# Retention's query-times-state product: two fp32 matmuls replaced by six fp32r matmuls on split operands

## The chip, the cores and the metric

The kernel runs on one core of a Trainium2 chip. TensorE (PE) multiplies matrices from SBUF into PSUM, VectorE (DVE) and ScalarE (ACT) do elementwise work on SBUF and PSUM, GpSimd (POOL) does elementwise work on SBUF, and SyncE (SP) mostly issues DMAs. Each engine runs its own instructions in order. The metric is the device time in microseconds (us); lower is better.

## The reference, cut to what matters

Two layers, each a mixer and a convolutional feed-forward network. Layer 0 mixes by a gated delta net, layer 1 by retention, which is the part that concerns us: 1024 tokens in 8 chunks of 128, 4 heads, keys of 256 and values of 512.

```python
scores = jnp.einsum('bhncd,bhnmd->bhncm', q, k) * dmask[None, :, None]
intra = jnp.einsum('bhncm,bhnmv->bhncv', scores, v)

def step(state, inp):
    q_n, k_n, v_n = inp
    o = jnp.einsum('bhck,bhkv->bhcv', q_n, state) * xi[None, :, :, None]
    state = (state * gamma_c[None, :, None, None]
             + jnp.einsum('bhck,bhcv->bhkv', k_n * zeta[None, :, :, None], v_n))
    return state, o

o = _unchunk_heads(intra + jnp.moveaxis(inter, 0, 2))
o = _standardize(o, 1e-6).reshape(b_, s, H * dv)
o = o * jax.nn.silu(gate.astype(F32))
return o.astype(h.dtype) @ w_out
```

The state is 256 x 512 per head. The product of the change is `q_n` (128 x 256) times `state`, once per chunk and head, from the second chunk on (the state starts at zero).

## The kernel before

**Split products.** Nearly all products are taken as three fp32r matmuls: an operand x is split into a high part (`act.activation(dst_h, src, AF.Copy)`, which rounds to fp32r, L89) and a low part (`eng.tensor_tensor(dst_l, src, dst_h, ALU.subtract)`, L90; `eng` is VectorE unless given), and low x high, high x low and high x high are summed in PSUM. `split` (L88) does this. A few products stay plain fp32 matmuls.

**Retention, layer 1.** Two streams share TensorE. `core(h)` runs through the chunks of head h; `ret_fill` makes the values V of the heads one half (four chunks) after the other (`ret_v`) and then the first two block products of the output projection (`proj_gen`). The planner `run` (L727) writes TensorE's order out by hand: a stream that yields a number is not continued before so much planned time has passed, a core step goes before fill, and the constants in `RL` are these pauses. `pm` and `ptr` pin each matmul and transpose behind the one before. The other engines' instructions take program order among what is ready.

**One chunk n of `core`**, in program order:

- the next state `Sn` (two halves j of 128 x 512): three fp32r matmuls each (`sc<-vv,kz`), then VectorE adds the decayed old state (L1957; for n = 0 it copies, L1955)
- `ret_front` for chunk n+1: scores (`mm<-qk`), transposes of k, `kz` (zeta times k, split, L1921 and L1922), the masked scores `sT` (L1924) and their split `sThl`; it also keeps the slices of q that the chunk needs
- a pause `RL["p"]`, then the output `po` (`sc<-vv,sThl`: three fp32r matmuls; for n > 0 also `sc<-Sr,qk`: two plain fp32 matmuls of q times the state `St`)
- `ret_back` starts as a stream of its own: statistics of `po` (L1977, L1979, L1980), a power on GpSimd (L1981), the normalised `on` (L1985), after a pause `RL["b"]` four transposes (`mm<-cst,on`), times the gate (L2006), and stores; from n = 4 on also four GpSimd operations that combine output blocks (L2017). For n < 4 it also starts a gain step (GpSimd, L2055 and L2056) for the residual input
- a pause `RL["c"]`

`po` and the state products take PSUM banks from the tag `sc`, which has two.

**The ring `qkv`** is an SBUF tag of 20 places of 128 x 512. A chunk's V takes two of them (`vv`, high and low). `take("qkv", 2)` in `ret_v` holds the fill back, in the plan, until two places are free, and `give("qkv", 2)` in `core` gives a chunk's two back; the count starts from `free["qkv"] = 20`. The output projection's blocks and weights use the same tag.

`load_qk` brings q and k of a head from DRAM into the tags `aux` and `auh`, each half as two tiles or two slices of one tile of 128 x 512.

Of the kernel before, what the change touches and what calls it, by code (L numbers as in the profile page):

```python
# [9 lines left out]
F32 = mybir.dt.float32  # L10
F32R = mybir.dt.float32r
# [4 lines left out]
P = 128  # L16
D = 1024
S = 1024
KT = D // P
HALF = 512  # L20
NCH = S // P
GH = 8
RH = 4
# [10 lines left out]
def trunk_kernel(ctx: ExitStack, tc, A):  # L34
# [6 lines left out]
    dr = ctx.enter_context(tc.tile_pool(name="dr", bufs=1, space=bass.MemoryType.DRAM))  # L41

    BUFS = {"hTa": 8, "hTb": 8, "qkv": 20, "aux": 4, "auh": 8, "lane": 4, "cv": 4, "ada": 1,
            "wr": 2, "wh": 2, "wl": 2, "t2": 3, "sm": 14, "sm2": 6, "st": 8, "s8": 6, "S": 6, "qx": 3, "fs": 1, "xT": 2}

    def tl(tag, shape, dt=F32, name=None):
        return sb.tile(shape, dt, tag=tag, name=name or tag, bufs=BUFS[tag])

    def two(tag, dt=F32, name=None):
        if tag in ("qkv", "auh"):  # L50
            return tl(tag, [P, HALF], dt, name), tl(tag, [P, HALF], dt, name)
        t = tl(tag, [P, 2, HALF], dt, name)
        return t[:, 0], t[:, 1]
# [7 lines left out]
    def mm_tile():  # L61
        return ps.tile([P, HALF], F32, tag="mm", name="mm", bufs=2)

    def sc_tile():
        return ps.tile([P, HALF], F32, tag="sc", name="sc", bufs=2)
# [16 lines left out]
    def hs(half):  # L82
        return slice(half * HALF, (half + 1) * HALF)
# [4 lines left out]
    def split(dst_h, dst_l, src, eng=dve):  # L88
        anchor["sp"] = act.activation(dst_h, src, AF.Copy)  # L89
        eng.tensor_tensor(dst_l, src, dst_h, ALU.subtract)  # L90
# [488 lines left out]
    xT = {}  # L579
# [118 lines left out]
    U, DT, R, St = {}, {}, {}, {}  # L698
# [6 lines left out]
    def pq(inst, cost):  # L705
        if pin[0] is not None:
            tc.add_manual_dep(inst.ins, pin[0].name,
                              mybir.DependencyInfo(mybir.DependencyClass.NoSync, mybir.DependencyReason.DATA),
                              reason="issue order")
        pin[0] = inst.ins  # L710
        clk[0] += cost
# [3 lines left out]
    def pm(out, lhsT, rhs, start=True, stop=True, cost=None):  # L715
        pq(pe.matmul(out, lhsT, rhs, start=start, stop=stop), cost or COST[out.shape[-1]])  # L716

    def ptr(out, src):
        pq(pe.transpose(out, src, ident), 0.109)

    def after_ev(*names):
        return ("ev", names)

    def emit(name, lat=0.0):
        events[name] = clk[0] + lat
# [43 lines left out]
    free = {"qkv": 20 - 2 * (len(first) - 1), "lane": 4, "aux": 0, "auh": 8, "t2": 3, "xT": 2}  # L769
# [6 lines left out]
    def give(tag, n):  # L776
        free[tag] += n
# [461 lines left out]
    for p in range(4):  # L1239
        q = p & 2  # L1240
# [668 lines left out]
    def ret_front(h, n, q, k):  # L1909
        s4 = slice(n % 4 * P, (n % 4 + 1) * P)  # L1910
        qh, kh = q[n // 4], k[n // 4]
        r = {}
        pk = mm_tile()
        p1 = pk[:, 2 * P:3 * P]
        for j in range(2):
            pm(p1, kh[j][:, s4], qh[j][:, s4], start=(j == 0), stop=(j == 1))
        if n < NCH - 1:
            for j in range(2):
                ptr(pk[:, j * P:(j + 1) * P], kh[j][:, s4])
            kz = r["kz"] = tl("t2", [P, 2, 2 * P], F32R, name="kz")  # L1920
            act.activation(kz[:, 0], pk[:, 0:2 * P], AF.Copy, scale=zeta[:, h:h + 1])  # L1921
            dve.scalar_tensor_tensor(kz[:, 1], pk[:, 0:2 * P], zeta[:, h:h + 1], kz[:, 0], ALU.mult, ALU.subtract)  # L1922
        sT = tl("S", [P, P], name="sT")
        dve.tensor_mul(sT, p1, dmask[:, h * P:(h + 1) * P])  # L1924
        sThl = r["s"] = tl("qx", [P, 2, P], F32R, name="sThl")
        split(sThl[:, 0], sThl[:, 1], sT)
        r["q"] = [qh[j][:, s4] for j in range(2)]
        return r

    def core(h):  # L1930
        yield after_ev(("rv", h, 0), ("core", h - 1))
        if h == 1:
            bg_ada(1, 2, "row")
        q, k = load_qk(h, 0), load_qk(h, 1)
        emit(("qk", h))
        St = None
        yield RL["q"]
        r = ret_front(h, 0, q, k)
        yield RL["f"]
        for n in range(NCH):  # L1940
            if n == 4:
                yield after_ev(("rv", h, 1))
            vh, vl = va[h][n]
            Sn = None
            if n < NCH - 1:
                kz = r["kz"]
                Sn = tl("lane", [P, 2, HALF], name="Sr")
                for j in range(2):
                    js = slice(j * P, (j + 1) * P)
                    p2 = sc_tile()  # L1950
                    pm(p2, kz[:, 1, js], vh, start=True, stop=False)
                    pm(p2, kz[:, 0, js], vl, start=False, stop=False)
                    pm(p2, kz[:, 0, js], vh, start=False, stop=True)
                    if n == 0:
                        dve.tensor_copy(Sn[:, j], p2)  # L1955
                    else:
                        dve.scalar_tensor_tensor(Sn[:, j], St[:, j], gamma_c[h], p2, ALU.mult, ALU.add)  # L1957
                    yield 0.0
                rn = ret_front(h, n + 1, q, k)
                yield RL["p"]  # L1960
            po = sc_tile()
            sT = r["s"]
            pm(po, sT[:, 1], vh, start=True, stop=False)
            pm(po, sT[:, 0], vl, start=False, stop=False)
            pm(po, sT[:, 0], vh, start=False, stop=(n == 0))
            if n > 0:
                for j in range(2):
                    pm(po, r["q"][j], St[:, j], start=False, stop=(j == 1), cost=0.857)
            give("qkv", 2)
            yield [(-0.1, ret_back(h, n, po))]  # L1970
            yield RL["c"]
            St, r = Sn, rn
        emit(("core", h))
# [46 lines left out]
    def load_qk(h, j):  # L2020
        out = []
        for hf in range(2):
            t = two(("aux", "auh")[j], F32, "qk")
            for d in range(2):
                sp.dma_start(t[d], qd[j, h, d][:, hs(hf)])
            out.append(t)
        return out

    RL = {"v": 2.57, "q": 5.9, "f": 3.35, "p": 0.55, "c": 2.75, "b": 3.21, "o": 4.42}
    va = [[] for _ in range(RH)]  # L2030

    def ret_fill():
        for h in range(RH):
            for half in range(2):
                yield from ret_v(h, half)
        while bg or pend:
            bg_step()
        for r in mix[0]:
            if r == "P2":
                return  # L2040
            yield r
# [27 lines left out]
    gbs = []  # L2069
    gains += [lambda m=m: gain_step(m) for m in range(2 * NCH + 1)]  # L2070
    events["core", -1] = clk[0]
    free["qkv"] = 20
    bg_tag[0] = "xT"
    run([(0.0, ret_fill())] + [(-1.0, core(h)) for h in range(RH)])
    bg_tag[0] = "wr"
    layer_tail(1, mix, None, xs[1], xs[2], A["out"], None, True)
# [102 lines left out]
```

## Time and profile before

| | us |
|---|---|
| median of 3 runs | 2877.69 |
| lowest, highest | 2877.47, 2882.09 |
| the profiled execution, first to last instruction (span) | 2868.4 |
| retention core within it | 1738 to 2050 |

The profiled execution's time is known only as its span; the runs' times include what lies around it. In the views an instruction group is given as line, engine, operation, `out<-in` by the program's tile names, shapes and count; then busy us, mean ns of one, and the engine's idle time before it with what ended it. In views by time the first two numbers are start and length in us. A plain fp32 matmul of 128x512 leaves two records, an fp32r one leaves one. The lengths of matmul records are modelled, so consecutive starts are the better measure of their cost.

### The profile page before, as it was taken

The page shows a single profiled execution, that of the slowest core. Times are in us where ns is not written, and L with a number is a line of the kernel's source. Part 1 is how long each engine was busy: PE and PEld are TensorE (multiplying, and loading weights), DVE is VectorE, ACT ScalarE, POOL GpSimd, SP SyncE. Part 2 cuts the span into 40 slices and gives each one's busy share as a digit, 9 for nine tenths or more (in the row PEclk, how much of TensorE's full clock was granted, in tenths as well). Part 3 has the DMA queues.
Part 4 walks back from the last instruction along what each step waited for, and adds up shares of the span by engine and source line. Part 5 has one row for each costly group of instructions (what it writes and reads, how often), then busy time and mean ns, then how long its engine had stood idle before and what let it go on. Part 6 is the DMA issues. An engine that isn't in the chain of part 4 may idle for free.

```text
span 2868.4 us, 38930 instructions
## 1 busy us (share of the span) xinstructions
PE 2780.8 (97%) x13594; PEld 2273.7 (79%) x13594; DVE 2177.9 (76%) x3874; ACT 1298.0 (45%) x2387; POOL 499.8 (17%) x513
## 2 busy tenths in 40 slices
PE   8999999999999999999999999999999999999997
PEld 6788878887787878887788887777777788888886
DVE  6787778676788888868687656666689887777779
ACT  4664465344645444545433342222344644445543
POOL 0311321000023322000000002333201033332201
PEclk9999999999999999999999999999999999999999
DMA  7223242174255554855343364665754253444753
GB/s 279 89 96 122 92 139 90 64 255 148 96 186 176 189 181 164 299 161 182 129 147 125 118 202 153 200 209 159 256 200 150 74 195 132 144 140 165 285 184 116
DMA packets 252884, 465.30 MB, mean 162 GB/s; under 512 B 24144, under 2 KB 77776, under 8 KB 252688
## 3 DMA queue, kind: packets, MB, share of 16 engines
q1 hardware_dynamic: 218560, 408.02, 43.0%
q10 hardware_dynamic: 31488, 46.15, 4.4%
q0 software_dynamic: 2640, 8.65, 0.8%
q8 instruction: 107, 1.75, 0.2%
q14 instruction: 89, 0.73, 0.1%
HBM read 346.86 MB, written 115.87 MB: 161 GB/s over the span
## 4 chain that ended last, share of the span: by engine, by line
PE 61%; DVE 20%; DMA 9%; ACT 5%; issue 4%; POOL 1%; SPq 0%; ACTq 0%; DVEq 0%; POOLq 0%
PE acc L716 11%; PE acc L1296 6%; PE acc L110 5%; PE acc L111 4%; PE acc L112 4%; PE sc L716 4%; PE sc L1296 3%; PE acc L1596 3%; PE mm L716 2%; DVE o L1742 2%; DVE wb L90 2%; PE sc L110 2%; PE sc L112 2%; PE sc L111 2%; DMA mvw<-in_ada_w 1%
## 5 line engine op out<-in xcount | busy, mean ns | idle before, releaser
L716 PE MATMUL acc<-hT,wh 128*128 128x512 f32 x960 | 299.4, 393 | 0.0
L1596 PE MATMUL acc<-bb,ab 128*128 128x512 f32 x984 | 229.7, 392 | 7.0 <-DVE ab L90 4.7
L89 ACT ACTIVATE ab<-ar 128x512 fp32r<-128x512 f32 x210 | 131.2, 630 | 221.3 <-PE mm L303 52.1
L1596 PEld LDWEIGHTS acc<-bb,ab 128*128 128x128 f32 x984 | 183.0, 188 | 49.0 <-DVE ab L90 4.2
L716 PEld LDWEIGHTS acc<-hT,wh 128*128 128x128 f32 x960 | 182.0, 190 | 35.5
L90 DVE TENSOR_TENSOR ab<-ar,ab 128x512 fp32r<-128x512 f32 x210 | 147.4, 707 | 76.5 <-ACT ab L89 76.3
L1296 PE MATMUL acc<-T,wb 128*128 128x512 f32 x840 | 202.0, 389 | 0.4 <-DVE wb L90 0.4
L89 ACT ACTIVATE wb<-mm 128x512 fp32r<-128x512 f32 x216 | 124.4, 597 | 166.0 <-DVE mm L1350 154.5
L716 PE MATMUL acc<-hT,wl 128*128 128x512 f32 x480 | 196.2, 409 | 2.2 <-ACT sq L509 2.2
L1296 PEld LDWEIGHTS acc<-T,wb 128*128 128x128 f32 x840 | 157.5, 188 | 33.8 <-ACT o L1743 1.2
L90 DVE TENSOR_TENSOR wl<-wr,wh 128x1024 fp32r<-128x1024 f32 x98 | 122.2, 1247 | 74.6 <-ACT wh L89 74.0
L1773 POOL TENSOR_TENSOR o<-o 128x512 f32<-128x512 f32 x80 | 126.2, 1586 | 266.4 <-ACT pc L1366 173.1
L90 DVE TENSOR_TENSOR wb<-wr,wb 128x512 fp32r<-128x512 f32 x162 | 115.3, 713 | 67.6 <-ACT wb L89 67.5
L89 ACT ACTIVATE wh<-wr 128x1024 fp32r<-128x1024 f32 x98 | 103.8, 1060 | 137.1 <-PE acc L716 56.4
L1742 DVE SCALAR_TENSOR_TENSOR o<-g,vc,o 128x512 f32<-128x512 f32 (+2 forms) x176 | 148.8, 855 | 8.4 <-ACT o L1737 7.1
L90 DVE TENSOR_TENSOR wb<-mm,wb 128x512 fp32r<-128x512 f32 x216 | 144.6, 682 | 7.8 <-ACT wb L89 7.8
L89 ACT ACTIVATE wb<-wr 128x512 fp32r<-128x512 f32 x162 | 101.1, 626 | 95.4 <-PE acc L1296 27.5
L1350 DVE TENSOR_TENSOR mm<-wr 128x512 f32<-128x512 f32 x108 | 83.6, 774 | 70.3 <-DMA wr<-in_ffn_up 57.7
L716 PE MATMUL acc<-wh,hT 128*128 128x512 f32 x384 | 134.3, 412 | 2.1 <-DVE vv L90 2.1
L1366 ACT ACTIVATE pc<-acc 128x512 f32<-128x512 f32 x143 | 84.5, 591 | 108.5 <-PE acc L1296 64.1
L239 DVE SCALAR_TENSOR_TENSOR ada<-mvw,e,ada 128x512 f32<-128x512 f32 x140 | 105.4, 753 | 24.9 <-DMA mvw<-in_ada_w 24.6
L110 PE MATMUL acc<-T,wb 128*128 128x512 f32 x292 | 114.4, 392 | 3.7 <-DVE wb L90 3.6
(675 smaller groups left out, 7343.0 us busy)
## 6 DMA issues: line engine op xcount, KB each, us to landing
wr<-in_ffn_up SPq DMA_DIRECT2D x92, 512.0 KB, 3.9
mvw<-in_ada_w SPq DMA_DIRECT2D x80, 512.0 KB, 4.3
ad<-o SPq DMA_DIRECT2D x154, 256.0 KB, 2.3
ar<-ad SPq DMA_DIRECT2D x154, 256.0 KB, 3.7
Br<-in_ffn_down SPq DMA_DIRECT2D x88, 256.0 KB, 3.6
wr<-in_ret_wv SPq DMA_DIRECT2D x32, 512.0 KB, 3.6
ar<-od SPq DMA_DIRECT2D x56, 256.0 KB, 5.2
wr<-in_gdn_wqkv SPq DMA_DIRECT2D x24, 512.0 KB, 3.6
```

Source lines behind the costliest of these rows:

```text
L89: anchor["sp"] = act.activation(dst_h, src, AF.Copy)
L90: eng.tensor_tensor(dst_l, src, dst_h, ALU.subtract)
L110: mm(acc, wl[:, k], hl[0], start=first, stop=False)
L111: mm(acc, wh[:, k], hl[1], start=False, stop=False)
L112: mm(acc, wh[:, k], hl[0], start=False, stop=last)
L239: dve.scalar_tensor_tensor(a, wr[:, kk], e[:, k:k + 1], a, ALU.mult, ALU.add)
L716: pq(pe.matmul(out, lhsT, rhs, start=start, stop=stop), cost or COST[out.shape[-1]])
L1296: return pe.matmul(*a, skip_group_check=True, **kw)
L1366: act.activation(t, X, AF.Copy)
L1596: return pe.matmul(*args, skip_group_check=True, **kw)
L1742: dve.scalar_tensor_tensor(tv, gv[:, c0 - j:c1 - j], w[:, 2 - j:3 - j], tv, ALU.mult, ALU.add)
L1773: (dve if fp == 0 else pool).tensor_tensor(o[d], o[x], o[y], op)
```

## The change

The two plain fp32 matmuls of q times state become six fp32r matmuls on split copies of both operands. The split is made one chunk ahead, by a new function `split_inter`, called for chunk n+1 right after `po` of chunk n. The split query `qs` is a new SBUF tag with one buffer; the split state `S2` takes four places of the ring `qkv`, whose count for values starts at 16 in place of 20. So that one instruction can split both 128-row parts of q, `load_qk` now takes a q half as one tile of 128 x 2 x 512 and keeps it in `qtile`.

```diff
-            "wr": 2, ..., "qx": 3, "fs": 1, "xT": 2}
+            "wr": 2, ..., "qx": 3, "fs": 1, "xT": 2, "qs": 1}
...
         split(sThl[:, 0], sThl[:, 1], sT)
-        r["q"] = [qh[j][:, s4] for j in range(2)]
         return r
+
+    def split_inter(h, n, q, Sn):
+        s4 = slice(n % 4 * P, (n % 4 + 1) * P)
+        qs = tl("qs", [P, 2, 2, P], F32R, name="qs")
+        qt = qtile[h][n // 4][:, :, s4]
+        split(qs[:, 0], qs[:, 1], qt)
+        S2 = [two("qkv", F32R, "S2") for _ in range(2)]
+        for j in range(2):
+            split(S2[j][0], S2[j][1], Sn[:, j])
+        return qs, S2
...
-        St = None
+        St = inter = None
...
             if n > 0:
+                qs, S2 = inter
                 for j in range(2):
-                    pm(po, r["q"][j], St[:, j], start=False, stop=(j == 1), cost=0.857)
+                    pm(po, qs[:, 1, j], S2[j][0], start=False, stop=False)
+                    pm(po, qs[:, 0, j], S2[j][1], start=False, stop=False)
+                    pm(po, qs[:, 0, j], S2[j][0], start=False, stop=(j == 1))
+            if Sn is not None:
+                inter = split_inter(h, n + 1, q, Sn)
             give("qkv", 2)
...
         for hf in range(2):
-            t = two(("aux", "auh")[j], F32, "qk")
+            if j:
+                t = two("auh", F32, "qk")
+            else:
+                whole = tl("aux", [P, 2, HALF], name="qk")
+                qtile[h].append(whole)
+                t = whole[:, 0], whole[:, 1]
...
+    qtile = [[] for _ in range(RH)]
...
-    free["qkv"] = 20
+    free["qkv"] = 16
```

More of the change, by code (lines that the diff above doesn't have):

```diff
@@ L43, in trunk_kernel @@
     BUFS = {"hTa": 8, "hTb": 8, "qkv": 20, "aux": 4, "auh": 8, "lane": 4, "cv": 4, "ada": 1,
-            "wr": 2, "wh": 2, "wl": 2, "t2": 3, "sm": 14, "sm2": 6, "st": 8, "s8": 6, "S": 6, "qx": 3, "fs": 1, "xT": 2}
+            "wr": 2, "wh": 2, "wl": 2, "t2": 3, "sm": 14, "sm2": 6, "st": 8, "s8": 6, "S": 6, "qx": 3, "fs": 1, "xT": 2, "qs": 1}
     def tl(tag, shape, dt=F32, name=None):
```

## The prediction

> **What bounds the kernel now.** I read the page's head first, then the busy time of the one stage that the change touches (from the first state product of head 0 to the last back-transposes of head 3, 1738 to 2050 us), then what TensorE waited for between 1733 and 2050 us.
>
> ```profile
> span 2868.4 us, 38930 instructions
> PE 2780.8 (97%) x13594; PEld 2273.7 (79%) x13594; DVE 2177.9 (76%) x3874; ACT 1298.0 (45%) x2387; POOL 499.8 (17%) x513
> 1738.00:2050.00 312.00, 307.66 (x1389) 235.94 (x1388) 209.07 (x382) 75.79 (x131) 106.38 (x119) 1.00 0.63 196
> PE sc L716 <- DVE on L1985: 2.8, 3, 1.9
> PE acc L716 <- DVE vv L90: 1.2, 3, 0.7
> PE mm L719 <- DVE on L1985: 0.4, 2, 0.2
> ```
>
> The third row is the stage: its length, the busy time of PE, PEld, DVE, ACT and POOL, then the granted clock, the DMA share and GB/s. TensorE is busy 307.66 of 312.00 us at a clock of 1.00, and its waits sum to 4.4 us. So TensorE's issue order is the bound, and time taken from TensorE is worth its length as long as VectorE, at 209.07 / 312 = 67%, still hands over in time. The handover that already stops TensorE most is `on` (L1985), the normalised output, which frees the PSUM bank of `po`.
>
> One chunk (head 1, n = 1), in order of time, shows how much room that handover has:
>
> ```profile
> 1828.82 0.86 PE L716 MATMUL sc<-vv,sThl 128*128 128x512 f32 x3
> 1829.52 1.88 PE L716 MATMUL sc<-Sr,qk 128*128 128x512 f32 x4
> ...
> 1830.88 0.29 DVE L90 TENSOR_TENSOR sThl<-sT,sThl 128x128 fp32r<-128x128 f32 x1 [0.72 <-ACT sThl L89]
> 1831.43 0.70 DVE L1977 BATCH_NORM_STATS2 rst<-sc 128x6 f32<-128x512 f32 x1 [0.26 <-PE sc L716]
> ...
> 1832.62 0.55 POOL L1981 TENSOR_TENSOR mv<-mv,mhalf 128x1 f32<-128x1 f32 x1 [1.62 <-DVE mv L1980]
> ...
> 1833.21 0.81 DVE L1985 TENSOR_SCALAR on<-sc,mv 128x512 f32<-128x512 f32 x1 [0.67 <-POOL mv L1981]
> ...
> 1834.19 1.28 ACT L89 ACTIVATE vv<-acc 128x512 fp32r<-128x512 f32 x2 [3.34 <-PE acc L716]
> ...
> 1834.67 1.52 PE L716 MATMUL sc<-vv,kz 128*128 128x512 f32 x6
> ...
> 1836.03 0.60 PE L716 MATMUL mm<-qk 128*128 128x128 f32 x4
> ```
>
> `po` ends, the statistics start at once (1831.43), and `on` ends at 1833.21 + 0.81 = 1834.02. The two state products of the next chunk are six fp32r matmuls in 1836.03 - 1834.67 = 1.36 us, 0.227 us each. There are two `sc` banks, so it is the second product, the fourth matmul, that takes the bank of `po`: at 1834.67 + 3 x 0.227 = 1835.35. So `on` is **1.33 us early**; whatever VectorE does before it is free up to there and stops TensorE beyond.
>
> **The change, part by part.**
>
> *TensorE.* Removed are two plain fp32 matmuls per chunk from n = 1 on, shown as four records:
>
> ```profile
> L716 PE MATMUL sc<-Sr,qk x112: 590/592/595, 1748.7 to 2048.3; 128*128 128x512 f32 x112
> 1799.60 1.88 PE L716 MATMUL sc<-Sr,qk 128*128 128x512 f32 x4
> 1801.32 0.60 PE L719 MATMUL mm<-cst,on 128*128 128x128 f32 x4
> ```
>
> 112 / 4 = 28 chunks, and one set takes 1801.32 - 1799.60 = 1.72 us. The last duration is modelled, so I take start to start. Added are six fp32r matmuls of 128x512 with 128x128 weights, the form of the state products above: 1.36 us. Saved: 28 x (1.72 - 1.36) = **10.1 us**. The fill between core steps is paced by the constants in `RL`, which do not change, so it stays and closes up.
>
> [...]
>
> *VectorE and ScalarE.* Each of the 28 chunks gets three splits: `qs` (128x256) and two halves of the state (128x512), all reading SBUF. Nearest rows:
>
> ```profile
> L90 DVE TENSOR_TENSOR ab<-ar,ab 128x512 fp32r<-128x512 f32 x9 | 6.7, 740 | 1.5 <-ACT ab L89 1.5
> L89 ACT ACTIVATE ab<-ar 128x512 fp32r<-128x512 f32 x9 | 5.7, 632 | 13.7 <-PE acc L716 12.5 <-DMA ar<-od 1.2
> L90 DVE TENSOR_TENSOR sThl<-sT,sThl x32: 269/293/1173, 1736.3 to 2042.1; 128x128 fp32r<-128x128 f32 x32
> L90 DVE TENSOR_TENSOR vv<-acc,vv x32: 677/691/693, 1722.6 to 2008.2; 128x512 fp32r<-128x512 f32 x32
> L2056 POOL TENSOR_TENSOR xg<-xg,gb 128x512 f32<-128x512 f32 x16 | 22.6, 1411 | 1.3
> ```
>
> A third of the way from 0.293 (128 columns) to 0.740 (512) gives 0.44 us for the `qs` subtraction. VectorE: 2 x 0.74 + 0.44 = 1.92 us a chunk, 54 us in all, so (209 + 54) / 302 = 87%. ScalarE: at most 3 x 0.63 = 1.9 us, 53 us on top of 76; it stays under half and I cost it at nothing.
>
> The 54 us are off the path only where VectorE idles ahead of `on`. They stand in program order before the statistics (L1977), so what is ready goes first, and `bn_stats`, aggregation, `on`, then `ot` queue behind. In the chunk above VectorE idles 0.72 + 0.26 = 0.98 us on the way to L1977; `po` will end 0.36 us sooner, which leaves 0.62. The delay of `on` is 1.92 - 0.62 = 1.30 us against a cover of 1.33 us: **the cover is just used up.**
>
> The sThl and vv rows say why it won't hold every time. The vv subtraction, with one operand in PSUM, never leaves 677 to 693 ns; the sThl one, with both in SBUF, goes from 293 up to 1173, 0.88 us more. All three new subtractions have both operands in SBUF, and GpSimd is busy 106.38 / 312 = 34% of the stage, with gain products of 1.41 us.
>
> [...]
>
> Expected per subtraction: 0.34 x 0.88 = 0.3 us, 0.9 us a chunk, in part behind other waits (`on` waits 0.67 us for GpSimd anyway). State products follow the chunks n = 0 to 5, so 4 x 6 = 24 places can stop. Bounds: nothing, if the delays fall into idle time; and, if no idle time is used, 1.92 + 0.88 - 1.33 = 1.47 us x 24 = 35 us. I take 0.25 us a place, 24 x 0.25 = **6 us**, near the lower end, since the quoted chunk gives zero and the collisions only part of 0.9.
>
> A second kind of chunk (n = 5) is late already:
>
> ```profile
> 1868.38 0.15 DVE L1980 TENSOR_SCALAR mv<-mv 128x1 f32<-128x1 f32 x1
> ...
> 1869.99 0.55 POOL L1981 TENSOR_TENSOR mv<-mv,mhalf 128x1 f32<-128x1 f32 x1
> 1870.57 0.81 DVE L1985 TENSOR_SCALAR on<-sc,mv 128x512 f32<-128x512 f32 x1 [2.03 <-POOL mv L1981]
> 1870.67 1.73 PE L716 MATMUL sc<-vv,kz 128*128 128x512 f32 x6
> ```
>
> GpSimd's power comes 1.46 us after its input, behind the four output operations of the chunk before. A VectorE delay of 1.30 us hides in that; the 0.21 us stop (1.73 against 1.52) stays.
>
> *The ring.* Values get 16 places, the state's two splits four. Live values at most: the `vv` row at 1834.19 is half 1 of head 1, with eight places of half 0 still held less the one or two chunks done, so 14 at most. Between heads TensorE does V alone until the next core starts:
>
> ```profile
> 1886.27 0.63 PE L719 MATMUL mm<-cst,on 128*128 128x128 f32 x4 [0.18 <-DVE on L1985]
> ...
> 1895.48 0.60 PE L716 MATMUL mm<-qk 128*128 128x128 f32 x4
> ```
>
> So the core waits for V, not V for places. I cost the ring at nothing; if it did hold V, TensorE would idle for up to this 8.6 us at each of three boundaries. `qs` has one buffer, so its copy on ScalarE waits for the end of `po`, with the next `wh`, `vv` and `kz` copies queued behind; ScalarE idles 3.34 us before the `vv` row, so nobody waits for that.
>
> **Sum.** 10.1 - 6 = 4.1 us off the span of 2868.4. The median is 2877.69, 9.3 us above this span; I keep that difference: 2877.7 - 4.1 = **2873.6 us**. About 0.2%, 5.8 us, is what a measurement of this kernel can tell from no change; the forecast falls just inside.
>
> **Rivals.**
> - *Full cover.* The subtractions sink into idle time; loss 0 to 3 us, so 2867.6 to 2870.6, say 2868.6. For it: 1.33 us of room and 33% idle VectorE. Against it: collisions, and n = 0, whose `po` has no state term and gets no shorter.
> - *VectorE becomes the bound (slower).* The mechanism is the queue ahead of L1977: once `on` is later than 1.33 us in the normal chunk, every further us is a stop at the second state product. The gain is gone at 10.1 / 24 = 0.42 us beyond cover; at 0.9, some two thirds of the upper bound, it is 24 x 0.9 - 10.1 = +11.5, so 2889 us. For it: 87% busy and program order. Against it: the splits are due only at the next `po`, several us later, so the order may put them after `on`.
> - *The gain is swallowed behind the last core.*
>
> ```profile
> 2052.40 0.69 DVE L1470 TENSOR_TENSOR Bw<-Br,Bw 128x512 f32<-128x512 f32 x1 [3.68 <-DMA Br<-in_ret_wout]
> PE mm L719 <- DVE on L1985: 3.8, 1, 3.8
> ```
>
> The second row is from the waits between 2000 and 2200 us. VectorE waits for a weight, the last statistics queue behind it, and TensorE stops 3.8 us. The out projection's loads share the ring, which has four places fewer; if they set the time, an earlier core waits longer, and up to all 10.1 us go: about 2877 us.
>
> **How the numbers follow.** Forecast (2870.6 to 2878) 0.50, full cover 0.27, VectorE bound 0.15, swallowed 0.08. Faster by over 0.2% (below 2871.9): full cover and 0.07 of the forecast, 0.34. Slower by over 0.2%: 0.15. Within: 0.51. The range is 2867 to 2882: full cover at the bottom, and 0.35 us a place more than the forecast (24 x 0.35 = 8.4) at the top; most of the VectorE case is left out.
>
> **What would show it.** Six `S2` matmuls in 1.36 us where four records took 1.72; 28 fewer x 0.36 us of PE time in the stage; VectorE some 54 us busier; waits of `sc` matmuls on `on` up from 2.8 to about 9 us. The forecast is wrong if that wait stays near 2.8 (full cover), passes 13 (slower), or if L716's `acc` matmuls begin to wait for ring places.

## The result and the profile after

The changed kernel is slower, by a little: ratio of its times to those of the kernel before 1.0038 [1.0026, 1.0049], about +10.9 us. The medians are 2888.32 us (seven runs, 2883.78 to 2894.05) and 2881.00 us (seven runs, 2871.44 to 2884.66). Forecast were 2873.6 us and a range up to 2882; the time lies outside, and on the side that had 0.15. The profiled execution took 2894.05 us, 1.75 us more than its span.

The page's head, after:

```profile
span 2892.3 us, 39206 instructions
PE 2784.0 (96%) x13650; PEld 2287.6 (79%) x13650; DVE 2234.9 (77%) x3958; ACT 1336.2 (46%) x2471; POOL 509.2 (18%) x513
```

The spans differ by 23.9 us, much more than the medians, because two executions drift apart ahead of the stage too. (Line numbers move with each edit: `on` is L1985 in the kernel before, L1999 in the changed one, and L1986, L1998 or L2004 in the versions below.) The stage itself is measured without that by the transposes of `on`, of which the first and the last mark nearly its whole length. The row gives count, shortest / median / longest record in ns, then first and last start. Before:

```profile
L719 PE MATMUL mm<-cst,on x128: 272/273/446, 1746.8 to 2057.3; 128*128 128x128 f32 x128
```

After:

```profile
L719 PE MATMUL mm<-cst,on x128: 270/273/421, 1755.9 to 2077.2; 128*128 128x128 f32 x128
```

From first to last start, 310.5 us became 321.3: +10.8, the whole of the measured difference. I call this the stage length from here on. 9.1 us of the two spans' difference was there before the stage began.

What TensorE waited for in the stage after (1742 to 2080 us; total us, times, longest):

```profile
PE acc L716 <- DVE vv L90: 5.7, 8, 1.8
PE sc L716 <- DVE Sr L1966: 5.2, 1, 5.2
PE acc L716 <- DVE mv L1994: 3.6, 3, 2.1
PE mm L719 <- DVE on L1999: 2.5, 3, 0.9
PE acc L716 <- DVE ab L90: 1.9, 2, 1.5
PE sc L716 <- DVE on L1999: 1.2, 4, 0.4
```

The rows sum to 20.1 us. The 4.4 us that the prediction has for before were read up to 2050 us only, but the last transposes of `on` belong to the stage, and TensorE stopped 3.80 us ahead of them:

```profile
2056.64 1.08 PE L719 MATMUL mm<-cst,on 128*128 128x128 f32 x4 [3.80 <-DVE on L1985]
```

So before has 8.2 us of waits in the same stage, and the change added 11.9.

The last of the six rows is the handover that the prediction priced: it **fell** from 2.8 to 1.2 us. The other 18.9 us stand at handovers that the prediction costed at nothing, above all the V accumulators (`acc` matmuls waiting for `vv`) and the state sum `Sr`. The rows of `mv` and `ab` are matmuls of the output projection (`acc<-bb,ab`); in the longest of them, at 2064.68, the subtraction of its operand `ab` ended at 2064.62 and a tiny `mv` at 2064.69, so I count both rows as that operand's.

TensorE's part is as announced. The six new matmuls and the next matmul behind them:

```profile
1848.71 1.55 PE L716 MATMUL sc<-S,qs 128*128 128x512 f32 x6
...
1850.10 0.39 PE L716 MATMUL acc<-wh,22_12810 128*128 128x512 f32 x1
```

1850.10 - 1848.71 = 1.39 us, where 1.36 was expected and 1.72 stood before: 28 x 0.33 = 9.2 us saved.

### The profile page after: what moved, and what is told of

Its sections match the earlier page's. It is cut to its first block, busy times and chain, and to the rows that moved or that the text cites. A ratio compares the mean times of both kernels' runs of the same rounds, so it can differ in the third digit from the quotient of the medians.

```text
span 2892.3 us, 39206 instructions
## 1 busy us (share of the span) xinstructions
PE 2784.0 (96%) x13650; PEld 2287.6 (79%) x13650; DVE 2234.9 (77%) x3958; ACT 1336.2 (46%) x2471; POOL 509.2 (18%) x513
## 4 chain that ended last, share of the span: by engine, by line
PE 57%; DVE 23%; DMA 9%; ACT 6%; issue 4%; POOL 1%; SPq 0%; ACTq 0%; POOLq 0%; DVEq 0%
PE acc L716 10%; PE acc L1296 5%; PE acc L1596 4%; PE acc L110 4%; PE acc L111 4%; PE acc L112 4%; PE sc L716 3%; PE sc L1296 3%; DVE o L1742 3%; PE mm L716 2%; DMA wr<-in_ffn_up 2%; DVE wb L90 2%; DVE qkv L490 2%; DMA mvw<-in_ada_w 2%; DVE mm L1350 2%
```

## Where the time goes: one takeover of V

When a half of V ends, four accumulators in PSUM have to be copied off (ScalarE `vv`, then VectorE's subtraction for the low part) before TensorE can start the next half. After, head 1; ScalarE and VectorE rows, then TensorE's two stops:

```profile
1842.46 0.40 ACT L89 ACTIVATE qs<-qk 128x256 fp32r<-128x256 f32 x1
1845.99 0.63 ACT L89 ACTIVATE S<-Sr 128x512 fp32r<-128x512 f32 x1 [3.12 <-DVE Sr L1966]
1847.08 0.47 ACT L1921 ACTIVATE kz<-mm,vc 128x256 fp32r<-128x256 f32 x1 [0.46 <-PE mm L719]
1847.45 0.62 ACT L89 ACTIVATE S<-Sr 128x512 fp32r<-128x512 f32 x1
1847.97 0.59 ACT L89 ACTIVATE vv<-acc 128x512 fp32r<-128x512 f32 x1
1848.55 2.07 ACTq L2024 DMA_DIRECT2D od<-ot  x2
...
1849.03 0.67 DVE L90 TENSOR_TENSOR S<-Sr,S 128x512 fp32r<-128x512 f32 x1
1849.63 0.67 DVE L90 TENSOR_TENSOR vv<-acc,vv 128x512 fp32r<-128x512 f32 x1
...
1850.94 0.58 ACT L89 ACTIVATE vv<-acc 128x512 fp32r<-128x512 f32 x1
...
1852.61 0.50 PE L716 MATMUL acc<-wh,hT 128*128 128x512 f32 x1 [0.99 <-DVE vv L90]
...
1855.40 0.51 PE L716 MATMUL acc<-wh,hT 128*128 128x512 f32 x1 [0.83 <-DVE vv L90]
```

Look at the second row. ScalarE is idle for 3.12 us, because the instruction at the head of its queue is the copy of the new state, and the state is not summed yet. Two accumulators are finished in that time; their copies stand behind it and start at 1847.97 and 1850.94. Between the two, ScalarE issues two stores, which hold it for 2.07 us; that part of the second copy's delay is not the state's. The same place in the version with the state's split moved behind the pause (`state_late`, below; its clock reads 5.8 us less at the same matmul):

```profile
1838.13 1.28 ACT L89 ACTIVATE vv<-acc 128x512 fp32r<-128x512 f32 x2 [1.01 <-PE acc L716]
1841.28 0.48 ACT L1921 ACTIVATE kz<-mm,vc 128x256 fp32r<-128x256 f32 x1 [1.87 <-PE mm L719]
```

Here both copies run at 1838.13, so at 1843.9 on the other's clock: four to six us earlier, the first of them in the very idle time that the state's copy had held. So in the changed kernel ScalarE idled 3.12 us ahead of the state's copy and took neither of the two ready copies behind it.

One row of the groups shows it for the whole stage (1742 to 2080 us): ScalarE's 28 copies of V and the idle time ahead of them. Before, after, then `state_late`:

```profile
L89 ACT ACTIVATE vv<-acc 128x512 fp32r<-128x512 f32 x28 | 16.7, 596 | 38.0 <-PE acc L716 37.2
```

```profile
L89 ACT ACTIVATE S<-Sr 128x512 fp32r<-128x512 f32 x56 | 35.3, 630 | 88.5 <-DVE Sr L1966 80.4 <-DVE Sr L1964 8.1
L89 ACT ACTIVATE vv<-acc 128x512 fp32r<-128x512 f32 x28 | 16.5, 591 | 3.7 <-PE acc L716 3.1
```

```profile
L89 ACT ACTIVATE S<-Sr 128x512 fp32r<-128x512 f32 x56 | 34.6, 629 | 49.0 <-DVE Sr L1969 40.3 <-DVE Sr L1967 8.7
L89 ACT ACTIVATE vv<-acc 128x512 fp32r<-128x512 f32 x28 | 16.7, 596 | 13.0 <-PE acc L716 12.1
```

Before, ScalarE stood ready for the accumulators (37.2 us of waiting for TensorE, at 14 of the copies' starts). After, it waited for them 3.1 us, 3 times: mostly it came late. Its idle time did not shrink by being used; it moved to the front of `S`, 80.4 us.

The largest single stop is a chunk of head 2, where VectorE, too, holds at the head of its queue for something else, a weight's DMA:

```profile
1945.98 0.75 DVE L239 SCALAR_TENSOR_TENSOR ada<-mvw,e,ada 128x512 f32<-128x512 f32 x1 [2.03 <-DMA mvw<-in_ada_w]
...
1947.25 0.68 DVE L90 TENSOR_TENSOR S<-Sr,S 128x512 fp32r<-128x512 f32 x1
...
1949.55 0.69 DVE L1991 BATCH_NORM_STATS2 rst<-sc 128x6 f32<-128x512 f32 x1
1950.16 0.87 DVE L90 TENSOR_TENSOR qs<-qk,qs 128x256 fp32r<-128x256 f32 x1
...
1953.75 0.67 DVE L1966 SCALAR_TENSOR_TENSOR Sr<-Sr,sc 128x512 f32<-128x512 f32 x1
...
1954.47 1.65 PE L716 MATMUL sc<-vv,kz 128*128 128x512 f32 x3 [5.23 <-DVE Sr L1966]
```

Before, TensorE stopped at this chunk too, for 1.90 us at 1937.06. With the new subtractions in the same queue (the rows of `S` and `qs`) it is 5.23.

## The experiments

Every ratio is to the kernel before, run beside it on the same chip. A ratio of 1.001 is 2.9 us. The stage lengths come from each profile's row of `on`'s transposes, as above (last start less first start); each is one execution, and they follow the ratios to within some 4 us.

| kernel | ratio | us | stage us (before 310.5) |
|---|---|---|---|
| after | 1.0038 [1.0026, 1.0049] | +10.9 | 321.3 |
| ring16 | 0.9994 [0.9984, 1.0005] | -1.7 | 312.8 |
| splits_only | 1.0054 [1.0042, 1.0066] | +15.5 | 323.6 |
| high_only | 1.0005 [0.9995, 1.0014] | +1.4 | 312.0 |
| split_late | 0.9990 [0.9979, 1.0001] | -2.9 | 307.0 |
| pe_only | 0.9969 [0.9957, 0.9980] | -8.9 | 300.2 |
| high_only_late | 0.9956 [0.9940, 0.9973] | -12.7 | 296.0 |
| q_late | 1.0033 [1.0022, 1.0045] | +9.5 | 320.3 |
| state_late | 0.9980 [0.9969, 0.9990] | -5.8 | 307.0 |
| late_pool | 1.0055 [1.0043, 1.0068] | +15.8 | 329.3 |
| late_pool_q | 0.9982 [0.9972, 0.9993] | -5.2 | 304.9 |
| state_late_pool_q | 0.9979 [0.9967, 0.9991] | -6.0 | 306.6 |
| state_late_pool_s | 0.9996 [0.9984, 1.0007] | -1.2 | 312.8 |

### The parts of the change: ring16, splits_only, high_only, pe_only

`ring16` is the kernel before with only the ring's count changed:

```diff
-    free["qkv"] = 20
+    free["qkv"] = 16
```

> The kernel before with the count of value places at 16 in place of 20, nothing else. VectorE theory (the three subtractions per chunk fill VectorE's queue, so that what TensorE waits for comes late): no change, within 3 us of before. Ring theory (V is held back for places): most of the +11 us of the change, +8 or more, with TensorE idle before acc matmuls.

No measurable change: the ring costs nothing, as the prediction had it. The `acc` matmuls that began to wait in the changed kernel do so for V's copies out of PSUM and for the output projection's operand, not for places.

`pe_only` is the kernel before with the product's matmuls replaced by six fp32r ones on operands that are at hand, without any split:

```diff
-                    pm(po, r["q"][j], St[:, j], start=False, stop=(j == 1), cost=0.857)
+                    for i in range(3):
+                        pm(po, sT[:, 0], vh, start=False, stop=(j == 1 and i == 2))
```

> The kernel before with the two fp32 matmuls replaced by six fp32r matmuls on tiles that are split already (scores and values), so the query times state product is left out and nothing is added on ScalarE and VectorE. If TensorE's saving of 28 x 0.36 us is real and comes through: -8 to -12 us against before. If it is taken back behind the core whatever the splits do (waits on loads of the output projection): -4 us or less.

-8.9 us by the times, -10.3 by the stage. TensorE's saving of about 10 us is real and reaches the end of the stage when nothing is added elsewhere.

`splits_only` is the changed kernel with its splits, but the product still as two fp32 matmuls:

```diff
-                    pm(po, qs[:, 1, j], S2[j][0], start=False, stop=False)
-                    pm(po, qs[:, 0, j], S2[j][1], start=False, stop=False)
-                    pm(po, qs[:, 0, j], S2[j][0], start=False, stop=(j == 1))
+                    pm(po, r["q"][j], St[:, j], start=False, stop=(j == 1), cost=0.857)
```

> The changed kernel with its splits, but q times state still as two plain fp32 matmuls; the splits are made and not read. VectorE theory: the stops of the change without its saving of 10 us, so about +20 us against before (+14 to +26). Theory that the new matmuls themselves are the cost: about +0 to +3 us.

+15.5 us without the saving. So the splits cost 15 to 20 us, where the prediction charged 6, and the loss doesn't need the shorter `po`. TensorE's largest wait in it:

```profile
PE sc L716 <- DVE on L1998: 7.8, 6, 4.0
```

With the long `po` the stops do come at `on`, near the 9 us that the prediction named, though 3.99 of the 7.8 are one stop, at the chunk of head 2 shown above. My reading is that the faster product shifted TensorE's stream against the others, and with it the handover that is late first; no run tests that alone.

`high_only` is the changed kernel without the low parts: the three subtractions are gone, ScalarE's three copies stay, and the six matmuls read high parts only.

```diff
-        split(qs[:, 0], qs[:, 1], qt)
+        act.activation(qs[:, 0], qt, AF.Copy)
...
-            split(S2[j][0], S2[j][1], Sn[:, j])
+            act.activation(S2[j][0], Sn[:, j], AF.Copy)
```

> The changed kernel without the low parts: the three VectorE subtractions per chunk are left out, and all six matmuls read the high parts. TensorE and ScalarE have the work of the change. VectorE theory: the saving comes through, -8 to -11 us against before, and TensorE's waits on VectorE in the stage fall to the level of before (some 4 to 9 us). ScalarE or ring theory: still slower than before by 5 us or more.

This missed. With all of VectorE's new work gone, the 10 us of saving still did not appear. It is what made me drop VectorE as the only cause and look at ScalarE's queue.

### The place of the splits: split_late, high_only_late, q_late, state_late

`split_late` moves the call behind the pause that follows `po`:

```diff
-            if Sn is not None:
-                inter = split_inter(h, n + 1, q, Sn)
             give("qkv", 2)
             yield [(-0.1, ret_back(h, n, po))]
             yield RL["c"]
+            if Sn is not None:
+                inter = split_inter(h, n + 1, q, Sn)
```

> The changed kernel with the splits for the next chunk one pause later in program order: behind the output statistics and the normalised output, ahead of the next state product. Same work on every engine. If the place in VectorE's order makes the loss: -3 to -9 us against before. If the sheer load of 54 us makes it: as the change, +6 to +14 us.

The same work at another place in the program order is worth 10.9 + 2.9 = 13.8 us. `high_only_late` is `high_only` with the same move, and so leaves out the low parts too:

> Late splits with the low parts left out (no VectorE subtraction, all six matmuls read high parts). If what high_only lost is ScalarE's order (its copies ahead of the values' copies when a half of V is taken over): -6 to -9 us against before, near pe_only. If ScalarE's copies cost whatever their place: 0 to -3 us, as high_only.

-12.7 us against +1.4: with no subtraction in the kernel, **the place of the copies alone is worth 14 us**. Against `pe_only` (-8.9), which has no copies, they cost 10 us at the early place and nothing at the late one. ScalarE's copies of V and TensorE's waits for them tell the same; `high_only`, then `high_only_late`:

```profile
L89 ACT ACTIVATE vv<-acc 128x512 fp32r<-128x512 f32 x28 | 16.5, 590 | 2.5 <-PE acc L716 2.0
PE acc L716 <- DVE vv L90: 5.2, 8, 1.2
```

```profile
L89 ACT ACTIVATE vv<-acc 128x512 fp32r<-128x512 f32 x28 | 16.7, 596 | 15.1 <-PE acc L716 14.2
PE acc L716 <- DVE vv L90: 1.2, 3, 0.7
```

That handover is 4.0 us of the 14. Another 5.13 us is a single stop of `high_only` at 2053.05, where the output projection's operand waited for its load (`ar<-od`); what made that load late isn't shown.

Which copy does it? The copy of q waits for the end of `po` (`qs` has one buffer), the state's copies wait for the state sum. `q_late` moves only q's split behind the pause, `state_late` only the state's:

```diff
             if Sn is not None:
-                inter = split_inter(h, n + 1, q, Sn)
+                iS = split_state(Sn)
             give("qkv", 2)
             yield [(-0.1, ret_back(h, n, po))]
             yield RL["c"]
+            if Sn is not None:
+                iq = split_inter(h, n + 1, q, Sn)
```

That is `q_late`; in `state_late` the two calls change places.

> After, with only the split of q moved behind the yield of RL["c"]; the state's split stays ahead of give. Theory A (ScalarE's copy of q, which waits for the end of the transpose in po, holds up the copies of the V half queued behind it): nearly the whole gain of the late place, ratio near split_late's 0.999, 0.998 to 1.001. Theory B (the state's copies and subtractions, the larger part, take the early place from other work): near after's 1.0038, 1.003 to 1.005. Theory C (each does its own share): 1.001 to 1.003.

> After, with only the split of the state moved behind the yield of RL["c"]; the split of q stays ahead of give. Theory A (q's copy): near after's 1.0038, 1.003 to 1.005. Theory B (the state's): 0.998 to 1.001. Theory C: 1.001 to 1.003. A and B cannot both hold here and in q_late.

The state's: `q_late` keeps the loss (+9.5), `state_late` is rid of it (-5.8). Theory A, that q's copy blocks ScalarE, is wrong. These two move the state's subtractions along with its copies; that the copies are what counts comes from the pair before.

### VectorE's share: late_pool, late_pool_q, state_late_pool_q, state_late_pool_s

At the late place the subtractions are still worth 12.7 - 2.9 = 9.8 us (11.0 by the stage). If that is VectorE's time, it should come back on GpSimd. `late_pool` is `split_late` with all three there:

```diff
-        split(qs[:, 0], qs[:, 1], qt)
+        split(qs[:, 0], qs[:, 1], qt, pool)
...
-            split(S2[j][0], S2[j][1], Sn[:, j])
+            split(S2[j][0], S2[j][1], Sn[:, j], pool)
```

> split_late with all three subtractions of a chunk moved from VectorE to GpSimd. If VectorE's time is what they cost (about 10 us, from high_only_late against split_late): ratio near 0.9956 to 0.997. If GpSimd takes longer than the pause leaves (its result is needed before the first product with the state), TensorE waits for qs or S in place of on: 1.000 to 1.010, and the waits name POOL L90.

+15.8 us; the second theory was right about the loss and wrong about the wait. `late_pool`, first what TensorE waited for, then GpSimd and the `on` that follows:

```profile
PE sc L716 <- DVE on L1999: 16.3, 10, 2.7
```

```profile
1848.51 0.15 DVE L1994 TENSOR_SCALAR mv<-mv 128x1 f32<-128x1 f32 x1
1849.84 1.28 POOL L2075 TENSOR_TENSOR xg<-xg,gb 128x512 f32<-128x512 f32 x1 [2.79 <-issue]
...
1851.08 0.74 POOL L90 TENSOR_TENSOR qs<-qk,qs 128x256 fp32r<-128x256 f32 x1
1851.78 0.55 POOL L1995 TENSOR_TENSOR mv<-mv,mhalf 128x1 f32<-128x1 f32 x1
...
1852.36 0.81 DVE L1999 TENSOR_SCALAR on<-sc,mv 128x512 f32<-128x512 f32 x1 [3.70 <-POOL mv L1995]
```

The power's own input was not late: this tiny instruction, which `on` needs, was ready at 1848.66 and ran at 1851.78. GpSimd idled up to 1849.84 ahead of a gain product (the profile shows nothing that it waited for), then ran that and the new subtraction of q, which is 0.70 us of these 3.12. In the changed kernel the same chunk's power ran ahead of that gain product (1843.96 and 1846.09), so here the new order of GpSimd's queue cost more than the subtraction's own length. In this version the handover that the prediction priced, `on` to the second state product, did become the largest wait, in this chunk by way of GpSimd's queue.

`late_pool_q` moves only q's subtraction to GpSimd, `state_late_pool_q` does that in `state_late`, and `state_late_pool_s` moves the second half of the state's in `state_late`.

> split_late with only the subtraction of q moved from VectorE to GpSimd. If VectorE's time is what counts: about a third of the 10 us comes back, ratio 0.998 from 0.999. If GpSimd is late: slower than split_late, with a wait on POOL for qs.

> state_late with the subtraction of q on GpSimd, still ahead of give. VectorE is relieved of 27 subtractions of 128x256 a stage; GpSimd takes about 0.78 us for each (row of late_pool_q), ahead of the same chunk's pow. Theory A (VectorE's time is what is left of the cost): ratio 0.996 to 0.998. Theory B (what delays on counts: pow waits behind the subtraction on GpSimd, as in late_pool): at or above state_late's 0.998, 0.998 to 1.002.

> state_late with the subtraction of the state's second half on GpSimd (1.35 us each in late_pool), late; the other two stay on VectorE. Theory A: VectorE relieved of 27 subtractions of 128x512, ratio 0.995 to 0.997. Theory B (GpSimd's queue reaches pow later behind it, as with all three in late_pool): 0.998 to 1.004, with waits on on in the windows where GpSimd's background adds run.

None differs from its own base by more than the intervals (0.9982 to 0.9990; 0.9979 and 0.9996 to 0.9980). So taking one subtraction off VectorE gains nothing that can be measured, and whether the 10 us are VectorE's time, or what the subtractions delay on whichever engine, **stays open**. `state_late_pool_s`, which of these three takes most off VectorE, came out as its theory B had it, but it also puts 1.40 us a chunk into GpSimd's queue (its 28 subtractions there averaged 1397 ns). Part of the 10 us can be placed: the chunk of head 2 shown above stops TensorE for 4.27 us in `split_late` and 1.02 in `high_only_late` (one profile each); its stop is 3.88 to 5.23 us in `after`, `splits_only`, `split_late` and `state_late`, and at most 2.81 in `before`, `pe_only` and the two `high_only` versions, which have no new subtractions. The late place does not mend that stop.

`state_late`, `late_pool_q` and `state_late_pool_q` beat both kernels, by 5 to 6 us against before and 16 to 17 against after, and can't be told from one another; `split_late` is faster than after, and its interval against before includes no change.

### A theory that fell: more cover after po

After the first results I thought that the shorter `po` had shortened the cover of `on`, and gave the fill more time behind it: the pause `c` from 2.75 to 3.44 in all three kernels.

```diff
-    RL = {..., "c": 2.75, "b": 3.21, ...}
+    RL = {..., "c": 3.44, "b": 3.21, ...}
```

> Late splits (as split_late), and the pause after the output product one fill step (three matmuls, 0.69 us) longer. Cover theory (the stops come because too little TensorE work lies between an output product and the next state product): -5 to -10 us against before. If the stops left in split_late are waits on loads and on the row sums of the background product: as split_late, -1 to -5 us.

> The kernel before with the same longer pause alone, as a control. Cover theory: little to gain, since TensorE waits only 4.4 us in the stage, 0 to -3 us against before.

> The changed kernel (splits right behind the output product) with the longer pause. Cover theory: 24 places x up to 0.69 us more room; the change's +11 us falls to between -4 and +5 us. If the loss comes from ScalarE and VectorE order where a half of V is taken over, room at this place does not help: +7 us or more.

All slower: 1.0065 [1.0053, 1.0077], 1.0041 [1.0029, 1.0053] and 1.0122 [1.0109, 1.0135]. The pause `c` had passed `b`, so the transposes of `on` came ahead of the next state product; TensorE's waits for them in `before_more_fill`, then in `after_more_fill`:

```profile
PE mm L719 <- DVE on L1985: 13.6, 12, 2.0
```

```profile
PE mm L719 <- DVE on L1999: 24.4, 23, 3.8
```

The pair confounds order with cover, so I raised `b` to 3.9 as well.

```diff
-    RL = {..., "c": 2.75, "b": 3.21, ...}
+    RL = {..., "c": 3.44, "b": 3.9, ...}
```

> The changed kernel with both pauses longer by one fill step (c 3.44, b 3.9), so that the back-transposes stay behind the next state products, as they are in the changed kernel. Cover theory (VectorE's handovers come late by less than one more fill step): -4 to +5 us against before. If the stops are at the places where a half of V is taken over and at loads: +7 us or more, as the changed kernel.

> Late splits with both pauses longer by one fill step. Cover theory: -6 to -10 us against before, the best so far without left-out work. Otherwise: as split_late, -1 to -5 us.

> The kernel before with both pauses longer by one fill step, a control. It waits 4.4 us in the stage, so 0 to -3 us against before by the cover theory.

1.0073 [1.0056, 1.0091], 1.0048 [1.0031, 1.0065] and 1.0045 [1.0028, 1.0063]: each is 10 to 17 us slower than the same kernel with the old pauses, the kernel before among them. More fill behind `po` doesn't mend the changed kernel; why it also slows the kernel before wasn't followed up.

## Why the prediction was wrong, point by point

- *TensorE saves 10.1 us.* Right: 9.2 by the rows after, 8.9 and 10.3 by `pe_only`.
- *VectorE gets 54 us, 1.92 us a chunk.* Nearly: the page shows 57.0 more. The two subtractions of the stage's groups after:

```profile
L90 DVE TENSOR_TENSOR S<-Sr,S 128x512 fp32r<-128x512 f32 x56 | 45.4, 811 | 1.3 <-ACT S L89 0.7
L90 DVE TENSOR_TENSOR qs<-qk,qs 128x256 fp32r<-128x256 f32 x27 | 15.2, 564 | 0.0
```

  A chunk costs 2 x 0.811 + 0.564 = 2.19 us, 0.27 more than the sum without collisions, where the prediction allowed up to 0.9 for them. What it calls a collision, a subtraction with both operands in SBUF that runs beside a GpSimd instruction, shows in the rows by time: after, the 32 of the 56 subtractions of the state that ran beside none took 0.67 to 0.69 us, the other 24 took 0.67 to 1.78, and the mean of all is 0.811, 0.13 above the 0.68 of those 32. The prediction's estimate for it, GpSimd's busy share times 0.88 us, was 0.3. V's 28, with one operand in PSUM, took 0.65 to 0.69, at least 10 of them beside GpSimd.
- *The stops come at `on` to the second state product, 24 x 0.25 = 6 us.* **This is the step that failed.** That wait went from 2.8 to 1.2 us. The prediction looked for one handover with a known margin of 1.33 us and put all of VectorE's new work against it; the margins of the other handovers (V's accumulators, the state sum, the back-transposes, the output projection's operands) were never worked out, and there stand 18.9 of the 20.1 us of waits. The 4.4 us of waits before were also read from a stage that the prediction let end at 2050; with the 3.80 us stop behind that they are 8.2.
- *ScalarE stays under half, "so nobody waits".* **Wrong, and the larger part of the loss: 14 us** by the place (`high_only` against `high_only_late`; `after` against `split_late`). The prediction saw the right hazard, a copy at the head of ScalarE's queue with `wh`, `vv` and `kz` behind it, but only for `qs`, where `q_late` and `state_late` show it harmless; the state's copies wait longer, for VectorE's sum. The 3.34 us of idle time ahead of `vv` that it took for cover was ScalarE standing ready for V; the state's copy took that place. How the 14 us divide over TensorE's handovers is known only in part.
- *The ring costs nothing.* Right (`ring16`).
- *The slower rival, 2889 us.* Its time fits the 2888.32, its mechanism doesn't: it had the loss at `on`, 0.9 us at each of 24 places, with the queue ahead of L1977. The sign that the prediction set for it (that wait over 13 us) did not appear; read by that sign alone, the profile would have said "full cover".
- *The gain is swallowed behind the last core, 2877 us.* No: in `pe_only` the saving came through, and in the changed kernel no stop at the transposes of `on` is longer than 0.9 us.
- *Full cover, 2868.6 us.* What the kernel would give if its splits cost nothing: `pe_only` took 2866.84 beside 2876.27 of the kernel before, 9.4 less, where this case had 9.1.

Not all of the loss stands in the waits. The stage is 321.3 - 300.2 = 21.1 us longer than in `pe_only`, whose waits in it are these (the row left out lies behind the stage):

```profile
PE mm L719 <- DVE on L1986: 4.5, 4, 3.5
...
PE sc L716 <- DVE on L1986: 1.8, 2, 1.0
PE acc L716 <- DVE vv L90: 1.4, 3, 0.6
```

7.7 us against 20.1, so 12.4 of the 21.1. Part of the rest is that a stop costs more than its idle time: around the one at 1852.61 three consecutive starts are 1851.23, 1852.61 and 1852.95, which is 1.26 us over two steps of 0.23, for 0.99 us shown. At that rate the 12.4 us would cost 3.4 more, and the some seven us of work at half clock (0.50 from 1954 to 1958 and from 2068 to 2071 us) below some 3.5 (estimates). That leaves some 2 us that I have not accounted for.

## What to carry to other kernels

An engine's idle time is cover only if it may be taken at any moment; before counting it, see what the idle engine stands ready for, and what will wait at the head of its queue in its place. Ask of a new instruction not only how long it runs but when its input is ready: issue it in program order behind what can run sooner. And when work goes onto an engine that serves several handovers, work out the margin of each, since the one that stops most today need not be the one that breaks.

## What the runs showed of the hardware

During the 5.23 us stop TensorE's granted clock fell, in windows of 4 us of the changed kernel (start:end, length, busy time of PE, PEld, DVE, ACT, POOL, clock, DMA share, GB/s):

```profile
1950.00:1954.00 4.00, 0.00 (x0) 0.00 (x0) 4.00 (x9) 0.00 (x0) 0.85 (x2) 0.72 0.46 138
1954.00:1958.00 4.00, 3.53 (x14) 3.24 (x14) 2.97 (x5) 1.66 (x3) 0.45 (x1) 0.50 0.86 262
1958.00:1962.00 4.00, 4.00 (x19) 3.27 (x18) 2.53 (x7) 0.73 (x2) 0.00 (x0) 0.93 0.23 66
1962.00:1966.00 4.00, 4.00 (x20) 3.34 (x19) 2.00 (x6) 1.06 (x1) 0.55 (x1) 1.00 0.22 66
```

```profile
1955.92 1.05 PE L716 MATMUL mm<-qk 128*128 128x128 f32 x4
```

Half speed for about four us of work, then full speed again: the three state matmuls at 1954.47, shown above, took 1955.92 - 1954.47 = 1.45 us, where three take 0.68 at 0.227 each. In the stage it fell once more, behind the stops that end at 2064.68 and 2067.19: 0.50 from 2068 to 2071 us. The length of a stop alone doesn't tell whether it falls: just behind the stage TensorE stopped for 2.11 us at the same matmul (`sc<-bb,ab`, L301) in both kernels. Before, where that stop ended at 2083.20, the clock read 1.00 in every window of 2 us from 2079 to 2091; after, where it ended at 2100.74, the clock read 0.50 from 2102 to 2104. So these traces give no length of stop from which on the clock falls.

Two stores issued from ScalarE's queue held it for 0.89 us in one chunk (1841.31) and 2.07 us in the next (1848.55, shown above); what made the second longer isn't shown. And the kernel before ranged over 13 us (2871.44 to 2884.66) in seven runs, so a difference of 3 us needs the interval, not two medians.
